# Four sums of squares from two rounded products each, a last token tile that ends in halves, and a new table of shifts

## The chip, the cores and the metric

The kernel runs on one core of a Trainium2 chip. The metric is the device time of one execution in microseconds (us); three timed runs of the kernel before are given below, and one further execution was profiled. TensorE (PE in the profile) multiplies, VectorE (DVE) and ScalarE (ACT) work on whole tiles of 128 partitions, GpSimd (POOL) and SyncE (SP) mostly start transfers. PEld is TensorE's loading of its stationary operand, which has its own records.

## The reference, cut to what matters

One layer of a diffusion backbone over 512 latent tokens and 256 context tokens, width 1024, all in float32:

```python
h = rms_norm(x, g_norm1) * (1.0 + sc1) + sh1
aq, ak, av, dq, dk, dv, dz, da, db, ga, gd = split_cols(h @ w_in)
y_attn = window_ctx_attention(q_a, k_a, v_a, k_ac, v_ac, attn_sink)
...
q_d, k_d, v_d = jnp.split(centred_short_conv(...), 3, axis=-1)       # with a silu
q_d = l2_normalize(heads(q_d, DN_HEADS)) * DN_HEAD_DIM ** -0.5       # 8 heads of 64
k_d = l2_normalize(heads(k_d, DN_HEADS))
o_dl, _, _ = bidir_delta(q_d, k_d, v_d, g, beta, s_cf, s_cb)         # chunks of 64 tokens
...
x_new = x + gt1 * (sigmoid(ga) * (y_attn @ w_br_attn) + sigmoid(gd) * (y_d @ w_br_dn)) @ w_out
out = x_new + gt2 * (square(relu(hm @ w_mlp1)) @ w_mlp2)
```

`l2_normalize` multiplies each head's 64 numbers with `rsqrt(sum of squares + 1e-6)`.

## The kernel before

**Layout.** Features stand on the 128 partitions and tokens along the columns until the last product. A product that needs float32 accuracy is made of three products of rounded operands (type fp32r): each operand is cut into an upper part `hi` and a rest `lo` by the helper `split` (one ACT copy with rounding, L231; one DVE subtraction, L232), and hi·hi, hi·lo and lo·hi are added up in one PSUM bank. A few small products are left in plain float32 (the trace has two records for each of them).

**The DeltaNet queries.** The 512 query features stand in four tiles `qT` of 128 x 512 (two heads each). In `rest`, `l2n` normalises one tile after another: ACT squares the tile (L785), one plain float32 product with `bones` (L788) sums the squares of each head, ACT takes Ln of the sums and Exp of minus half of it (L189), DVE multiplies the query with it (L795). `bones` is a 128 x 128 matrix of zeros and ones, one block of ones for each head; it is also used for the keys (`l2n` on 768 columns), for the attention's norms (L573) and for one sum of gates (L868).

**What runs beside it.** `rest` is woven with the four context steps of the DeltaNet recurrence (`chain_step`, whose products of 64 x 64 are at L1250), with the inversion of the triangular matrices on DVE (`invert`, L979 and L980) and with a `filler`: the products of the attention's branch (L1201) and of the gates (L1155). The eight latent steps of the recurrence follow, then the norm of its output (L1446), its transposes (L1451) and the product with `w_br_dn`.

**The last product.** `Flat.run` makes the last quarter of the MLP's second product: for each half `n` of the 1024 output columns, four banks `z` for four tiles of 128 tokens, and 4 pieces of weights x 2 x 3 products of 512 columns for each tile (L1876 to L1878). Each finished bank is multiplied with the gate's row (L1885), added to what the other three quarters left (L1887), and written to memory by SP (L1888).

**Order.** `arrange` lays the instructions of every engine in an order that is worked out when the program is built: `Lists.run` walks through them with its own costs and always takes the ready instruction of the lowest rank. The rank is the place in the program text, and each entry of `SHIFTS` (engine or -1 for all, first place, end, distance) moves the ranks of a range. Buffers come from one `Arena` that hands out places in a ring from `mem.ptr`; a place that is used again makes its new user wait for the old one.

Of the kernel before, what the change touches and what calls it, by code (L numbers as in the profile page):

```python
# [10 lines left out]
F32 = mybir.dt.float32  # L11
F32R = mybir.dt.float32r
BF16 = mybir.dt.bfloat16
AF = mybir.ActivationFunctionType
ALU = mybir.AluOpType
# [31 lines left out]
P = 128  # L47
D = 1024
KT = D // P
SEQ = 512  # L50
# [71 lines left out]
def tile_layer(ctx: ExitStack, tc: tile.TileContext, I: dict, out: bass.AP, dbg=None):  # L122
    nc = tc.nc
    V, A, G, PE = nc.vector, nc.scalar, nc.gpsimd, nc.tensor
# [5 lines left out]
    mats = ctx.enter_context(tc.tile_pool(name="mats", bufs=1))  # L130
# [5 lines left out]
    def nm(s):  # L136
        uid[0] += 1
        return f"{s}_{uid[0]}"

    mem = Arena(lambda o, n: nc.alloc_sbuf_tensor_at(nm("m"), [P, n], F32, offset=base + o * 4).ap(), 256, NU)  # L140
# [6 lines left out]
    alloc, bank = mem.get, lambda n=1: banks.get(n * 512)  # L147
# [3 lines left out]
    def load(out, key, *at):  # L151
        d = nc.sync.dma_start(out=out, in_=I[key][at] if at else I[key])
        if lastload:
            tie(d.ins, lastload[0].ins.name)
        return d

    def cload(key, shape, pool=const):
        t = pool.tile(list(shape), F32, name=f"c_{key}")
        load(t, key)
        return t  # L160
# [5 lines left out]
    r32 = lambda ap: ap.bitcast(F32R)  # L166
# [10 lines left out]
    def tie(later, name, how=nosync):  # L177
        tc.add_manual_dep(later, name, how, reason="order")
        ties.append((later.name, name))

    def act(out_, in_, func, **kw):

        sets = TABLES.get(func)
        if sets and actg["set"] not in sets:
            head = A.preload_act_table_set(sets[0])
            for o in actg["ops"]:
                tie(head.ins, o.name)
            actg.update(set=sets[0], head=head.ins, ops=[head.ins])
        r = A.activation(out_, in_, func, **kw)  # L189
        if sets:  # L190
            tie(r.ins, actg["head"].name)
            actg["ops"].append(r.ins)
        return r
# [258 lines left out]


    ident = cload("ident", [P, P], mats)
    bones = cload("bones", [P, P], mats)
    identb = mats.tile([P, P], BF16, name="identb")
    V.tensor_copy(identb, ident)
    maskb = mats.tile([P, 2, P], BF16, name="maskb")
# [77 lines left out]
    def wnext():  # L536
        w = wn.pop(0)
        if wq:
            wn.append(wq.pop(0)())
        return w  # L540
# [240 lines left out]
    def l2n(y, scale, parts, eps):  # L781

        n = parts[-1][1]
        t = alloc(n)
        A.activation(t.ap, y, AF.Square)  # L785
        for lo, hi in parts:
            ss = bank()
            PE.matmul(ss[:, :hi - lo], bones, t[:, lo:hi], start=True, stop=True)  # L788
            act(t[:, lo:hi], ss[:, :hi - lo], AF.Ln, bias=eps)
            ss.free()  # L790
        act(t.ap, t.ap, AF.Exp, scale=-0.5)
        if scale == 1.0:
            V.tensor_tensor(y, y, t.ap, op=ALU.mult)
        else:
            V.scalar_tensor_tensor(y, y, scale, t.ap, op0=ALU.mult, op1=ALU.mult)  # L795
        t.free()
# [10 lines left out]
    t, t2 = alloc(TOK), alloc(TOK)  # L807
# [249 lines left out]
    def mats():  # L1057
        for q in range(4):
            l2n(kT[q].ap, 1.0, ((0, SEQ), (SEQ, TOK)), epsc)
            yield  # L1060
        for gi in range(3):
            yield from chunk_mats(gi)
# [282 lines left out]
    def rest():  # L1345
        for q in range(4):
            l2n(qT[q].ap, HD ** -0.5, ((0, SEQ),), epsc4)
            yield
        for g in (1, 2):
            to_tokens(VTM, vT, g)  # L1350
            yield
        for t in vT:
            t.free()
        for g in (1, 2):
            to_tokens(KTM, kT, g)
            yield
# [18 lines left out]
    for g in range(2):  # L1375
        ms = slice(16 * g, 16 * g + 16)
        f, b = xa[0][:, ms], xa[1][:, ms]
# [9 lines left out]
    for g in range(2):  # L1387
# [20 lines left out]
        for a in range(2):  # L1408
            lo, hi = quad(a, 0), quad(a, 1)
# [38 lines left out]
    for qq in range(2):  # L1448
# [3 lines left out]
        for a in range(2):  # L1452
            n = 2 * qq + a
            t = alloc(512)
# [15 lines left out]
    for ct in range(8):  # L1470
        w = wnext()
# [32 lines left out]
    for ct in range(8 - NHALF):  # L1504
        w = wnext()
# [329 lines left out]
    class Flat:  # L1835
# [27 lines left out]
        def run(self):  # L1863

            self.ready.append(next(self.made))
            for n in range(2):
                z = [bank() for _ in range(4)]
                for p in range(4):
                    if len(self.parts) < 4:
                        self.left()  # L1870
                    hi, lo = self.parts[p]
                    wh, wl = self.ready.pop(0)
                    for tt, zz in enumerate(z):
                        c = slice(tt * P, tt * P + P)
                        for k in range(2):
                            PE.matmul(zz.ap, hi[:, k, c], wh[:, k], start=(p == k == 0), stop=False)  # L1876
                            PE.matmul(zz.ap, hi[:, k, c], wl[:, k], start=False, stop=False)  # L1877
                            PE.matmul(zz.ap, lo[:, k, c], wh[:, k], start=False, stop=(p == 3 and k == 1))  # L1878
                    m = next(self.made, None)
                    if m:  # L1880
                        self.ready.append(m)
                for tt, zz in enumerate(z):
                    cols, r = slice(n * 512, n * 512 + 512), tt % 2 * 512
                    y, t = alloc(512), ends[f"{1 + tt // 2}{1 + n}"][:, r:r + 512]
                    V.tensor_tensor(y.ap, zz.ap, grow[0][:, cols], op=ALU.mult)  # L1885
                    zz.free()
                    V.tensor_tensor(t, t, y.ap, op=(ALU.add, ALU.subtract)[n])  # L1887
                    nc.sync.dma_start(out=out[tt][:, cols], in_=t)  # L1888
                    y.free()

    def gather():

# [24 lines left out]
    ends = {}  # L1917
    grow = []
# [5 lines left out]
    for hf in range(4):  # L1924
        for f in range(0 if hf else FT):
            if first:
                bufs, _, acc = first.pop(0)
            else:
                bufs = [alloc(1024), alloc(1024)]
                w = wload(I["wm1"][f], bufs=bufs)  # L1930
                acc = bank()
                mm3(acc.ap.rearrange("p (n t) -> p n t", n=2), w, ms)
            r = alloc(512)
# [175 lines left out]
class Lists:  # L2109
# [177 lines left out]


SHIFTS = (
    (-1, 3553, 4764, 98), (-1, 3512, 3594, 1006), (-1, 7403, 7446, -155), (-1, 1987, 1996, 101), (0, 2046, 2292, -17),  # L2290
    (-1, 6044, 6077, -106), (0, 2023, 2126, -10), (-1, 115, 426, -27), (-1, 3445, 3672, -1637),
    (-1, 1527, 1528, 1489), (-1, 6310, 6694, -52), (-1, 1462, 1509, -625), (0, 2939, 2999, -93),
    (-1, 2608, 2663, 1010), (2, 3601, 4703, 34), (-1, 7250, 8101, -33), (0, 1850, 1939, 203), (-1, 2383, 2384, 17500),
    (-1, 3674, 3774, -4398), (0, 677, 698, -656), (-1, 3082, 3203, -110118), (-1, 2293, 2400, -38),
    (0, 6368, 6391, 130), (1, 4083, 4115, 18), (0, 2284, 2614, 138), (0, 2832, 2895, 504), (-1, 6541, 6601, -172),
    (1, 5748, 5839, -1941), (-1, 6770, 6908, 5), (0, 1571, 1968, -41), (-1, 82, 309, 175), (0, 6907, 7054, -30),
    (-1, 6985, 6999, 100), (0, 333, 759, 687), (2, 6255, 6839, 92), (-1, 2338, 2928, -326), (0, 5230, 5288, 60),
    (0, 6605, 6630, -34), (2, 6286, 6635, 1090), (0, 1833, 2823, -52), (-1, 3067, 3168, -1479), (0, 6835, 7284, -25),
    (-1, 6617, 6991, 6), (-1, 2334, 2705, -850), (1, 2045, 2628, 25751), (1, 2966, 3000, 88), (-1, 1888, 1979, 54),
    (-1, 6683, 6694, -12), (0, 4982, 5022, -19), (-1, 4895, 4909, -322), (2, 4328, 4389, -910), (2, 3659, 3660, -79),  # L2300
    (0, 3816, 4086, -547), (2, 3616, 3661, 426), (-1, 2698, 2889, -283), (-1, 791, 795, -1080), (-1, 4468, 4565, -70),
    (-1, 2662, 2768, 153), (0, 4688, 4730, 677), (-1, 1453, 2428, 57), (0, 3513, 3676, 1376), (-1, 2538, 2557, -85),
    (2, 3307, 3572, -734), (-1, 4301, 4316, 1562), (-1, 8021, 8081, -103), (0, 6446, 6490, -40), (-1, 6515, 6522, 73),
    (0, 4612, 4652, 330), (2, 2868, 2901, -688), (1, 6422, 6428, 63), (0, 7237, 7252, -31), (2, 3468, 3519, 1105),
    (0, 3385, 3512, -60), (0, 3767, 3844, -440), (-1, 3889, 4042, -388), (-1, 2356, 2379, -340), (0, 4054, 4254, -37),
    (1, 2710, 3030, -12), (-1, 3938, 4538, 65), (1, 1906, 1916, -331), (0, 2607, 2757, -420), (-1, 4509, 4514, 38),
    (1, 4064, 4220, -270), (0, 4178, 4479, -520), (0, 4039, 4130, 255), (0, 2791, 2991, -300), (1, 1978, 2978, -9),
    (-1, 7512, 8112, -45), (0, 1814, 1875, -81), (-1, 7228, 7238, -9), (0, 4201, 4254, 1120), (0, 4218, 4249, -885),
    (1, 3798, 4198, 186), (-1, 4320, 4327, -8), (0, 2876, 3156, 18), (0, 3295, 3371, -6), (-1, 3570, 4170, -472),
    (-1, 4087, 4267, -15), (-1, 2701, 2752, 63), (0, 3821, 4137, -80),  # L2310
)


# [120 lines left out]
```

## Time and profile before

| | us |
|---|---|
| median of three runs | 851.46 (850.16 to 853.5) |
| the profiled execution | 848.21 |
| its span, from the first to the last instruction | 846.4 |
| PE busy in the span | 833.7 |
| DVE busy | 699.2 |
| ACT busy | 534.2 |

The profiled execution has 1.81 us outside its span. PE is busy 98% of the span; PE records overlap one another (a record of 389 ns is followed by the next after some 227 ns), so where the profile gives the chain of work, the time from one product to the next is read there and not from the mean record. The granted clock is 1.00 in every 20 us of the span up to 840, which is TensorE's upper level of 2.4 GHz.

### The profile page before, as it was taken

What the parts mean: (1) busy time and instruction counts of PE and PEld (TensorE: products, weight loads), DVE (VectorE), ACT (ScalarE), POOL (GpSimd) and SP (SyncE); (2) the same over time, 40 slices, a digit from 0 to 9 for tenths busy, and PEclk for the clock granted to TensorE, in tenths of its full rate; (3) what the DMA queues carried; (4) which work ended last, traced back from release to release, by engine and by line L of the source; (5) the groups of instructions that cost most, each with busy time, mean ns of one, the idle gap of its engine ahead of it and who ended that gap; (6) DMA issues with size and microseconds to landing.
All of it is one profiled execution on the core that took longest, in us unless ns stands there. A gap on an engine that the chain in (4) does not pass through costs nothing.

```text
span 846.4 us, 18086 instructions
## 1 busy us (share of the span) xinstructions
PE 833.7 (98%) x7464; PEld 698.4 (83%) x7464; DVE 699.2 (83%) x1153; ACT 534.2 (63%) x920; POOL 60.3 (7%) x81
## 2 busy tenths in 40 slices
PE   8999999999999999999999999999999999999997
PEld 5688778887877778787778899888998899889986
DVE  5875999988779998868849879798689988989853
ACT  5568785487769896587754345398557447646520
POOL 0000011010000002000000000110011001111300
PEclk9999999999999999999999999999999999999999
DMA  9924365543221237643116755959259636998271
GB/s 367 369 76 100 76 151 124 124 85 70 38 38 31 62 116 243 213 141 103 41 41 246 241 161 190 312 131 264 95 157 194 169 129 162 187 269 229 35 190 50
DMA packets 38178, 127.31 MB, mean 150 GB/s; under 512 B 4688, under 2 KB 5200, under 8 KB 38096
## 3 DMA queue, kind: packets, MB, share of 16 engines
q1 hardware_dynamic: 30176, 99.43, 34.3%
q0 software_dynamic: 7920, 26.74, 18.6%
q8 instruction: 58, 0.95, 0.5%
q14 instruction: 24, 0.20, 0.1%
HBM read 118.29 MB, written 4.19 MB: 145 GB/s over the span
## 4 chain that ended last, share of the span: by engine, by line
PE 92%; DMA 5%; ACT 1%; DVE 1%; SPq 0%; issue 0%; ACTq 0%
PE banks L1619 14%; PE banks L1155 14%; PE banks L335 9%; PE banks L337 9%; PE banks L339 9%; PE banks L1809 4%; PE banks L1807 4%; PE banks L1808 4%; PE banks L1250 3%; PE banks L1201 3%; DMA m<-in_wada 2%; PE banks L732 2%; PE banks L1876 2%; PE banks L1878 2%; PE banks L1877 2%; DMA wr<-in_win 1%
## 5 line engine op out<-in xcount | busy, mean ns | idle before, releaser
L1619 PE MATMUL banks<-m,m 128*128 128x256 f32 x1008 | 126.2, 284 | 0.7 <-ACT m L231 0.7
L1619 PEld LDWEIGHTS banks<-m,m 128*128 128x128 f32 x1008 | 123.6, 192 | 2.9 <-ACT m L231 1.6
L231 ACT ACTIVATE m<-m 128x512 fp32r<-128x512 f32 (+2 forms) x123 | 90.9, 761 | 52.7 <-PE banks L1808 8.6
L232 DVE TENSOR_TENSOR m<-m,m 128x512 fp32r<-128x512 f32 (+2 forms) x123 | 103.0, 854 | 15.2 <-ACT m L231 12.9
L335 PE MATMUL banks<-m,wh 128*128 128x512 f32 (+1 forms) x312 | 112.1, 363 | 0.0
L337 PE MATMUL banks<-m,wh 128*128 128x512 f32 (+1 forms) x312 | 110.2, 355 | 0.0
L339 PE MATMUL banks<-m,wl 128*128 128x512 f32 (+1 forms) x312 | 109.6, 354 | 0.0
L1155 PE MATMUL banks<-m,wh 128*128 128x512 f32 x320 | 104.4, 401 | 1.3 <-ACT m L189 1.3
L299 ACT ACTIVATE wh<-wr 128x1024 fp32r<-128x1024 f32 (+1 forms) x60 | 56.6, 944 | 47.8 <-DMA wr<-in_wout 13.9
L1155 PEld LDWEIGHTS banks<-m,wh 128*128 128x128 f32 x320 | 59.2, 188 | 14.3 <-ACT m L189 1.8
L335 PEld LDWEIGHTS banks<-m,wh 128*128 128x128 f32 x312 | 58.9, 189 | 8.5 <-issue 0.5
L337 PEld LDWEIGHTS banks<-m,wh 128*128 128x128 f32 x312 | 59.0, 189 | 8.2 <-issue 0.5
L339 PEld LDWEIGHTS banks<-m,wl 128*128 128x128 f32 x312 | 58.9, 189 | 8.1 <-DVE wl L304 0.2
L1807 PE MATMUL banks<-wh,m 128*128 128x512 f32 x168 | 65.4, 392 | 0.0
L1808 PE MATMUL banks<-wl,m 128*128 128x512 f32 x168 | 65.2, 390 | 0.0
L1155 PE MATMUL banks<-m,wl 128*128 128x512 f32 x160 | 64.4, 404 | 0.4 <-DVE wl L304 0.4
L1809 PE MATMUL banks<-wh,m 128*128 128x512 f32 x168 | 64.4, 391 | 0.0
L304 DVE TENSOR_TENSOR wl<-wr,wh 128x1024 fp32r<-128x1024 f32 (+1 forms) x44 | 45.1, 1024 | 13.3 <-ACT wh L299 13.2
L335 PE MATMUL banks<-m,m 128*128 128x256 f32 (+1 forms) x136 | 45.6, 341 | 0.6 <-ACT m L344 0.5
L231 ACT ACTIVATE wh<-m 128x1024 fp32r<-128x1024 f32 x30 | 31.6, 1055 | 22.8 <-DMA m<-in_wm 15.5
L1733 POOL DMA_DIRECT2D m<-in_wm x24 | 20.8, 920 | 348.9 <-PE banks L339 167.2
L337 PE MATMUL banks<-m,m 128*128 128x256 f32 (+1 forms) x136 | 44.9, 337 | 0.1
(298 smaller groups left out, 1814.1 us busy)
## 6 DMA issues: line engine op xcount, KB each, us to landing
m<-in_wada SPq DMA_DIRECT2D x48, 512.0 KB, 5.0
wr<-in_win SPq DMA_DIRECT2D x38, 512.0 KB, 3.8
m<-in_wm SPq DMA_DIRECT2D x36, 512.0 KB, 4.9
wr<-in_wm SPq DMA_DIRECT2D x28, 512.0 KB, 4.5
m<-in_wm POOLq DMA_DIRECT2D x24, 512.0 KB, 7.6
wl<-in_win POOLq DMA_DIRECT2D x16, 512.0 KB, 6.0
m<-in_xT SPq DMA_DIRECT2D x8, 512.0 KB, 4.8
wr<-in_wbr SPq DMA_DIRECT2D x16, 256.0 KB, 2.6
```

Source lines behind the costliest of these rows:

```text
L231: A.activation(r32(hi), src, AF.Copy)
L232: (eng or V).tensor_tensor(r32(lo), src, hi, op=ALU.subtract)
L299: upper[0] = A.activation(r32(hi), raw, AF.Copy)
L304: V.tensor_tensor(r32(lo), raw, hi, op=ALU.subtract)
L335: PE.matmul(acc, w[0][:, k, :], xhi, start=(start and i == 0), stop=False)
L337: r = PE.matmul(acc, w[0][:, k, :], xlo, start=False, stop=(end and w[1] is None))
L339: r = PE.matmul(acc, w[1][:, k, :], xhi, start=False, stop=end)
L1155: PE.matmul(acc.ap, w[x][:, k, :], hx[k][y], start=(k == p == 0), stop=(k == KT - 1 and p == 2))
L1619: PE.matmul(dst, r32(self.w[w][i][:, k * P:(k + 1) * P]), xs7[x][k][j], start=(n == 0), stop=(n == 11))
L1807: PE.matmul(zz, hi[:, kk, ts_], wh[:, k], start=(kk == 0), stop=False)
L1808: PE.matmul(zz, hi[:, kk, ts_], wl[:, k], start=False, stop=False)
L1809: PE.matmul(zz, lo[:, kk, ts_], wh[:, k], start=False, stop=(kk == 3))
```

## The change

- `l2n` on 512 columns, the queries alone, cuts the squares into an upper part and a rest (`split`, into a place `up` that `aside` takes without moving the arena's pointer), and sums them by two fp32r products with `bones` (`head_sums`) in place of one float32 product. The keys' calls, with 768 columns, stay as they are.
- `bones` is loaded into a buffer of the arena and copied by ACT with the rounding type. Its load no longer goes through `load`, which ties a load behind the last of the `wada` loads.
- In the second half of `Flat.run` the last tile of 128 tokens has two banks of 256 columns instead of one of 512. Its 24 products of 512 columns become 48 of 256, and it is multiplied, added and written in two halves.
- `SHIFTS` is another table (99 entries after 103).

```diff
-    bones = cload("bones", [P, P], mats)
+    bones = mats.tile([P, P], F32, name="bones")
+    b_ = alloc(256)
+    nc.sync.dma_start(out=b_[:, :P], in_=I["bones"])
+    A.activation(r32(bones), b_[:, :P], AF.Copy)
+    b_.free()
+    def aside(n):
+        at = mem.ptr
+        b = alloc(n)
+        mem.ptr = at
+        return b
+    def head_sums(dst, hi, lo):
+        PE.matmul(dst, r32(bones), r32(hi), start=True, stop=False)
+        PE.matmul(dst, r32(bones), r32(lo), start=False, stop=True)
...
         A.activation(t.ap, y, AF.Square)
+        up = aside(2 * n) if n == SEQ else None
+        if up:
+            split(t.ap, up[:, :n], up[:, n:])
         for lo, hi in parts:
             ss = bank()
-            PE.matmul(ss[:, :hi - lo], bones, t[:, lo:hi], start=True, stop=True)
+            if up:
+                head_sums(ss[:, :hi - lo], up[:, lo:hi], up[:, n + lo:n + hi])
+            else:
+                PE.matmul(ss[:, :hi - lo], bones, t[:, lo:hi], start=True, stop=True)
...
-                z = [bank() for _ in range(4)]
+                z = [bank() for _ in range(4 + n)]
...
+                        if n and tt == 3:
+                            for h, zz in ((slice(0, 256), z[3]), (slice(256, 512), z[4])):
+                                for k in range(2):
+                                    PE.matmul(zz[:, :256], hi[:, k, c], wh[:, k, h], start=(p == k == 0), stop=False)
+                                    PE.matmul(zz[:, :256], hi[:, k, c], wl[:, k, h], start=False, stop=False)
+                                    PE.matmul(zz[:, :256], lo[:, k, c], wh[:, k, h], start=False, stop=(p == 3 and k == 1))
+                            continue
...
+                    w = 256 if n and tt == 3 else 512
+                    for o in range(0, 512, w):
+                        cols, t = slice(n * 512 + o, n * 512 + o + w), ends[f"{1 + tt // 2}{1 + n}"][:, at + o:at + o + w]
+                        V.tensor_tensor(y[:, o:o + w], z[tt + o // 256][:, :w], grow[0][:, cols], op=ALU.mult)
+                        V.tensor_tensor(t, t, y[:, o:o + w], op=(ALU.add, ALU.subtract)[n])
+                        nc.sync.dma_start(out=out[tt][:, cols], in_=t)
...
 SHIFTS = (
-    (-1, 3553, 4764, 98), (-1, 3512, 3594, 1006), (-1, 7403, 7446, -155), (-1, 1987, 1996, 101), (0, 2046, 2292, -17),
...
+    (-1, 3520, 4770, 98), (0, 7434, 7460, -59), (-1, 1995, 1996, 114), (-1, 2051, 2666, -45), (0, 2023, 2257, -108),
...
```

For the highest places the table before has `(-1, 8021, 8081, -103)`, the new one `(-1, 8046, 8342, -150)`; each `l2n` of a query, `bones` and the last tile together add some 40 instructions to the program.

## Rows read from the trace of the kernel before

**Rows 1.** The page: busy time by engine, and the chain's shares by engine.

```profile
PE 833.7 (98%) x7464; PEld 698.4 (83%) x7464; DVE 699.2 (83%) x1153; ACT 534.2 (63%) x920; POOL 60.3 (7%) x81
...
PE 92%; DMA 5%; ACT 1%; DVE 1%; SPq 0%; issue 0%; ACTq 0%
```

**Rows 2.** Busy time in four stretches, columns in the first line.

```profile
core 0: us, PE busy (x) PEld busy (x) DVE busy (x) ACT busy (x) POOL busy (x), PEclk, DMA share, GB/s
0.00:45.00 45.00, 40.38 (x290) 27.43 (x291) 31.93 (x73) 24.68 (x44) 0.21 (x4) 1.00 0.88 346
259.00:300.00 41.00, 40.26 (x331) 30.72 (x330) 39.97 (x72) 36.74 (x74) 0.00 (x0) 1.00 0.23 64
...
819.90:841.70 21.80, 21.79 (x97) 17.70 (x95) 8.38 (x11) 2.12 (x2) 0.00 (x0) 1.00 0.21 83
841.70:846.40 4.70, 0.00 (x0) 0.00 (x0) 1.38 (x2) 0.00 (x0) 0.00 (x0) 0.89 0.14 56
```

**Rows 3.** The chain in order of time: start us, us, line, products.

```profile
275.60 0.86 PE banks L788 x2
...
280.06 1.91 PE banks L788 x4
...
290.26 0.86 PE banks L788 x2
...
348.60 1.73 PE banks L901 x122
...
425.93 13.94 PE banks L1155 x60
...
601.93 32.75 PE banks L1619 x273
```

**Rows 4.** Timeline of ACT, PE and DVE, 259 to 300 us: start, us.

```profile
259.80 0.63 ACT L785 ACTIVATE m<-m 128x512 f32<-128x512 f32 x1
...
275.44 1.02 PE L788 MATMUL banks<-m,c_bones 128*128 128x512 f32 x2
...
293.95 0.68 DVE L795 SCALAR_TENSOR_TENSOR m<-m,m 128x512 f32<-128x512 f32 x1
```

**Rows 5.** Groups by form on ACT and DVE: count, busy us, mean ns.

```profile
L231 ACT ACTIVATE m<-m 128x512 fp32r<-128x512 f32 x76 | 46.3, 625 | 40.0 <-DMA m<-in_wm 8.4 <-DVE m L1610 8.3 <-DVE m L1477 6.1
...
L232 DVE TENSOR_TENSOR m<-m,m 128x512 fp32r<-128x512 f32 x76 | 51.1, 685 | 5.3 <-ACT m L231 4.8
...
L1307 DVE TENSOR_TENSOR m<-m,banks 128x256 f32<-128x256 f32 x20 | 8.1, 418 | 8.5 <-PE banks L1250 8.4
...
L1633 DVE TENSOR_TENSOR m<-m 128x256 f32<-128x256 f32 x12 | 5.0, 419 | 0.0
```

**Rows 6.** Timeline of the end of the span.

```profile
837.65 0.69 DVE L1885 TENSOR_TENSOR m<-banks,m 128x512 f32<-128x512 f32 x1 [2.66 <-PE banks L1878]
...
841.30 0.39 PE L1878 MATMUL banks<-wh,m 128*128 128x512 f32 x1
841.73 0.69 DVE L1885 TENSOR_TENSOR m<-banks,m 128x512 f32<-128x512 f32 x1 [2.66 <-PE banks L1878]
842.45 0.69 DVE L1887 TENSOR_TENSOR m<-m,m 128x512 f32<-128x512 f32 x1
...
843.17 0.33 SPq L1888 DMA_DIRECT2D out<-m  x1
```

**Rows 7.** Transfers from 842.4 to 846.4 us, 40 slices of 0.1 us.

```profile
GB/s 0 0 0 0 0 0 0 0 0 0 0 0 0 0 0 0 369 389 369 389 492 389 205 21 0 0 0 0 0 0 0 0 0 0 0 0 0 0 0 0
...
out<-m SPq DMA_DIRECT2D x1, 256.0 KB, 2.0
```

**Rows 8.** Timeline of PE and DVE after the recurrence, 414 to 452 us.

```profile
423.68 1.16 PE L1250 MATMUL banks<-m,m 64*64 64x64 f32 x64
...
439.71 0.71 PE L1451 MATMUL banks<-c_ident,m 128*128 128x128 f32 x5
...
430.88 2.36 DVE L1446 TENSOR_TENSOR m<-m,oss 128x1024 f32<-128x1024 f32 x2 [0.65 <-ACT oss L189]
```

## What the change will do: the prediction

> **What bounds the kernel now.** I read the page's totals first. PE is busy 833.7 of 846.4 us, and the chain that ended last runs 92% through PE [rows 1]. So the first question is not which engine to relieve but where PE stands still, and how much PE work the change removes. The windows answer the first half. Of the 846.4 − 833.7 = 12.7 us without a product, 45.00 − 40.38 = 4.6 lie in the first 45 us, where the DMA engines are 88% busy and the core waits for its inputs, and 4.7 lie behind the last product [rows 2]. That leaves 3.4 us in 797. In the middle, then, a microsecond of PE work that goes away is a microsecond of span, as long as no other engine has become the next limit there. DVE is the candidate: in the 41 us in which the queries are normalised it is busy 39.97 us, and ACT 36.74 [rows 2].
>
> Two paces are needed, and both come from the chain in order of time, since records overlap. Products of 512 rounded columns follow each other by 13.94 / 60 = 0.232 us with their neighbours' disturbances, and by 21.80 / 96 = 0.227 in the undisturbed last half [rows 2, 3]. Products of 256 columns, each with a stationary operand of its own, go by 32.75 / 273 = 0.120 us [rows 3].
>
> **The sums of squares.** One float32 product over 512 columns is two records and takes 0.86 us of the chain; there are four: 0.86 + 1.91 (two together) + 0.86 = 3.63 us [rows 3]. The pair in the middle lies between two groups of 64 x 64 products, and some 0.19 of its 1.91 is above two single ones: that is switching, which may stay. So 3.44 to 3.63 us go. Eight products of 512 rounded columns come, at 0.232: 1.86 us. PE has 1.6 to 1.8 us less to do; I take 1.7.
>
> Each query also gets an ACT copy of 0.625 us and a DVE subtraction of 0.685 [rows 5]: 2.5 and 2.7 us in all, in a stretch where ACT had 4.3 us free and DVE 1.0 [rows 2]. Two things could wait for that. First the product itself, which stands in PE's order with everything else behind it. In the trace a query's square starts at 259.80 and its product at 275.44, 15 us later [rows 4]; the next three have 13 to 20 us. The 1.3 us more fit in. The last scaled query is there at 294 and the products that need the queries start at 348.6 [rows 3, 4]. Second, the inversion, with which these subtractions share DVE: it ends up to 2.7 us later, and with it the latent recurrence. That recurrence has cover. Its last products come at 423.68 + 1.16 = 424.8, the norm of its output is done at 430.88 + 2.36 = 433.2, and the transposes that need it stand at 439.71, behind gate products that fill PE meanwhile [rows 8]. So 6.5 us of delay cost nothing, and I cost the DVE work at nothing. Without that cover it would cost 2.7.
>
> **Bones.** The load is the same 64 KB; the rounding copy has 128 columns, less than the 0.625 us of 512 [rows 5], and falls in the first 45 us or just behind, where ACT is busy 24.68 of 45 us [rows 2]. Nothing, then. Losing the tie to the `wada` loads matters only if SP puts this load ahead of one of them: at 346 GB/s [rows 2], 64 KB are 0.2 us. That is the upper bound.
>
> **The last tile.** On PE 24 x 0.227 = 5.45 us become 48 x 0.120 = 5.76: +0.31. Behind the last product the trace has the multiplication at 841.73, the addition at 842.45, and SP's issue at 843.17 [rows 6]: two DVE operations of 0.69 in a row. With 256 columns they take 0.42 each [rows 5], so −0.54, if the first half is out of the way. The evictions show that it is: they stand 841.73 − 837.65 = 4.08 us apart [rows 6], that is 18 products of 0.227 and not 6, so the order finishes a tile's last three weight pieces before it turns to the next tile. If the new order treats the two halves likewise, the first is finished 18 x 0.120 = 2.2 us before the end, and its 0.84 us of DVE work and its own SP issue of 0.33 are over by then. If the halves end together instead, four operations of 0.42 take 1.68 where two took 1.41: +0.27 instead of −0.54. The new table moves the program's end forward as the old one does, so I take −0.54. The last transfer moves 256 KB in 0.75 us (seven and a half slices), out of 2.0 from issue to landing [rows 7]; half the bytes give −0.37 at this pace, and nothing if the pace halves with the shorter rows. I take −0.37. The fifth bank is the one that the first half of the columns leaves first; it is wanted 18 products, 4.1 us, into the second half, and one DVE operation of 0.69 frees it [rows 6]: nothing.
>
> The tail is −0.54 − 0.37 + 0.31 = −0.6 us, between −0.6 and +0.6.
>
> The 273 products at 0.120 us each have a load of the stationary operand of their own [rows 3], and a load's record is 17.70 / 95 = 0.186 us [rows 2], so the loads lie under the products. A rule speaks against that and against the change. The Trainium skill, in "TensorE: Matmul & The Clock Gate", section "Part 3: Packing small matmuls — row/col tiling", says that loads overlap running products only when their row groups differ, which whole-array products don't; its section "LDWEIGHTS (loading the stationary operand)" gives 128/1.2, about 107 ns, for a load, so that 24 further loads would cost an estimated 2.6 us and the sum would be about +0.3 instead of −2.3. The trace's pace of 0.120 doesn't agree with that rule; it agrees with Part 2 of the same page, which also lets a load run ahead into a background buffer.
>
> **The shifts.** This is the cost that no row shows. The new order can at best win the 3.4 us that PE stands still in the middle; the 4.6 us at the start are bound by the bytes of the inputs. It can lose wherever a product is put ahead of its operand, and at the start, where a 512 KB load that is put ahead of a needed one costs 0.5 MB / 346 GB/s = 1.5 us [rows 2]. No row says which of the two tables fits the chip better. I take zero, in the middle between ends that lie alike far off, and ±2 us around it.
>
> **Sum.** −1.7 − 0.6 = −2.3 us. Against the profiled execution's own 848.21 that is 845.9. The three runs' median, 851.46, stands 3.25 above that execution, more than the change is worth; moved by the same −2.3 it is 849.2, and that is my number, a ratio of 0.9973. Half a per cent, 4.3 us, is about what a measurement of this kernel can tell from no change, so the likeliest verdict is no change.
>
> **Rivals.**
>
> *The new order also wins the idle time.* PE's 3.4 us in the middle go too: −5.7, 845.8 us. For it: outside the start and the tail nothing but the order keeps PE waiting. Against it: there is little left to win, and it would have to win more than 2.0 of the 3.4 to pass half a per cent. Chance 0.17, most of it beyond that line.
>
> *PE isn't what sets the time there.* DVE is 97% busy in that stretch and gets 2.7 us more [rows 2, 5]. If what PE gains is given back at the next wait for DVE, only the tail stays: −0.6, 850.9 us. Against it: the 6.5 us of cover. Chance 0.12.
>
> *Slower: the recurrence comes late.* One mechanism: the new order lays the inversion and the recurrence so that the last group of 64 x 64 products falls behind its 424.8. Up to 6.5 us later costs nothing [rows 8]; from there each microsecond is one of span with PE standing still before the transposes. Past 6.5 + 2.3 = 8.8 us the kernel is slower than before, past 13 by over half a per cent. DVE's 2.7 us alone don't reach the first of these points, but from 348.6 to 424.8 [rows 3, 8] the recurrence and what it needs are 76 us of handed-on steps. At 13 us: 855.7 us. Chance 0.08.
>
> *The loads of the halves aren't hidden.* Then 24 x 0.186 = 4.5 us more stand in the tail [rows 2], +2.2 in all: 853.7 us. Against it: the pace of 0.120 [rows 3]. It is the rule of the Trainium skill's Part 3, above, as a mechanism. Chance 0.02.
>
> **How the numbers follow.** The forecast has the rest, 0.61, with ±2 us of its own from the order and the tail. Faster by over 0.5%: 0.14 of the first rival and 0.03 from the forecast's edge, 0.17. Slower by over 0.5%: the late recurrence, 0.08, and 0.01 for a disturbed start: 0.09. Within: 0.74. The range reaches down to 845.0, which takes in the first rival's time, and up to 853.0, past the second; outside lie the slower case, the loads and the edges.
>
> **What would show it.** In the changed kernel's profile: eight products with `bones` of about 0.23 us in the chain and no float32 pair of 0.86 for the queries; the four subtractions on DVE, and an inversion that ends up to 2.7 us later while the transposes at L1451's new line still follow PE work; the last tile at a pace of 0.12; the 1.5 us from the last product's end at 841.7 to SP's last issue become 0.9; a last transfer that lands in about 1.6. PE busy should fall by 1 to 2 us. The forecast is wrong if the idle time of PE in the middle is far from 3.4 us, if the start of the first weight tile moves, or if the transposes wait for the recurrence.

## The result, and the profile after

The changed kernel takes 854.74 us (median of 14 runs, 851.8 to 859.7); the kernel before, in 14 runs beside it, 850.27 (848.8 to 854.05). The ratio is 1.0050, with a 95% interval of 1.0036 to 1.0065: 4.5 us slower by the medians, where −2.3 was forecast and 853.0 was the range's upper end. The profiled execution after took 854.03 us with a span of 852.3. That of before, 848.21, is the fastest of all its runs here, so the two profiles stand 5.8 us apart, 1.3 more than the medians. (The table of shifts has 92 entries after 100, not 99 after 103 as said above.)

The page after answers to [rows 1]; the windows and the transfer at the end answer to [rows 2, 7]:

```profile
PE 836.1 (98%) x7488; PEld 700.8 (82%) x7488; DVE 702.2 (82%) x1159; ACT 535.8 (63%) x925; POOL 59.9 (7%) x81
...
PE 83%; DVE 6%; DMA 5%; ACT 4%; issue 1%; DVEq 0%; ACTq 0%
```

```profile
0.00:45.00 45.00, 40.46 (x284) 26.73 (x285) 31.26 (x73) 24.69 (x44) 0.21 (x4) 0.96 0.89 346
...
848.30:852.30 4.00, 0.00 (x0) 0.00 (x0) 0.85 (x2) 0.00 (x0) 0.00 (x0) 0.85 0.26 98
...
out<-m SPq DMA_DIRECT2D x1, 128.0 KB, 1.8
```

PE has less to do and is busy 2.4 us longer; the chain, 92% PE before, now goes through DVE and ACT for a tenth of its length. Behind the last product stand 4.0 us where 4.7 stood. Of the queries' sums, the chain in order of time (start us, us, line) shows what was forecast, rounded products of 0.23 (of the eight, one starts with 0.26 and two stand at 0.43); DVE's timeline of the end answers to [rows 6]:

```profile
278.89 0.26 PE banks L469
279.15 0.23 PE banks L470
...
286.38 0.43 PE banks L469
```

```profile
846.89 0.69 DVE L1919 TENSOR_TENSOR m<-m,m 128x512 f32<-128x512 f32 x1
848.31 0.42 DVE L1918 TENSOR_TENSOR m<-banks,m 128x256 f32<-128x256 f32 x1 [0.73 <-PE banks L1904]
848.77 0.42 DVE L1919 TENSOR_TENSOR m<-m,m 128x256 f32<-128x256 f32 x1
```

So the edits look right one by one, and the time was lost elsewhere. Where, the same windows of before and after show (columns as in [rows 2]: length, then PE, PEld, DVE, ACT, POOL busy). Before:

```profile
260.00:300.00 40.00, 39.26 (x326) 29.93 (x325) 38.97 (x70) 35.74 (x72) 0.00 (x0) 1.00 0.23 66
300.00:340.00 40.00, 40.00 (x722) 32.06 (x721) 35.58 (x59) 31.48 (x67) 5.18 (x10) 1.00 0.58 184
340.00:380.00 40.00, 39.46 (x743) 31.29 (x745) 30.46 (x59) 27.57 (x65) 3.12 (x6) 1.00 0.55 176
700.00:740.00 40.00, 40.00 (x247) 36.13 (x247) 38.14 (x45) 27.79 (x33) 6.93 (x8) 1.00 0.82 181
780.00:820.00 40.00, 40.00 (x248) 35.87 (x247) 29.68 (x41) 18.76 (x26) 7.10 (x8) 1.00 0.44 95
```

After:

```profile
260.00:300.00 40.00, 38.65 (x296) 30.23 (x295) 39.50 (x69) 37.91 (x79) 0.00 (x0) 1.00 0.23 66
...
340.00:380.00 40.00, 38.79 (x732) 30.53 (x732) 31.70 (x59) 28.19 (x65) 4.51 (x9) 1.00 0.57 188
700.00:740.00 40.00, 38.26 (x247) 34.57 (x247) 34.69 (x43) 26.44 (x32) 6.15 (x8) 1.00 0.73 161
780.00:820.00 40.00, 39.55 (x263) 36.17 (x262) 30.05 (x40) 21.64 (x28) 7.11 (x8) 1.00 0.45 105
```

PE stands still 0.6 us more at 260 to 300, 0.7 at 340 to 380, 1.7 at 700 to 740 and 0.5 at 780 to 820: 3.5 of the 5.9 us between the spans, and 0.6 more lie at 45 to 260 us. The other 2.4 are PE's longer busy time, and the tail gives 0.7 back. In this execution the start takes 1.6 of the 2.4: the granted clock is 0.96 over the first 45 us where before has 1.00, on 40.46 us of PE work. That clock is not the reason for the loss: five of the changed kernel's runs have a mean granted clock of 1.00, and their median is 854.72 too. Which other records are longer, and why, isn't settled.

### The profile page after: what moved, and what is told of

Same layout as the page of the kernel before. It is cut to its first block, busy times and chain, and to the rows that moved or that the text cites. A ratio compares the mean times of both kernels' runs of the same rounds, so it can differ in the third digit from the quotient of the medians.

```text
span 852.3 us, 18149 instructions
## 1 busy us (share of the span) xinstructions
PE 836.1 (98%) x7488; PEld 700.8 (82%) x7488; DVE 702.2 (82%) x1159; ACT 535.8 (63%) x925; POOL 59.9 (7%) x81
## 4 chain that ended last, share of the span: by engine, by line
PE 83%; DVE 6%; DMA 5%; ACT 4%; issue 1%; DVEq 0%; ACTq 0%
PE banks L1179 12%; PE banks L335 10%; PE banks L337 9%; PE banks L339 9%; PE banks L1643 8%; PE banks L1833 4%; PE banks L1832 4%; PE banks L1831 4%; DMA m<-in_wm 3%; PE banks L1274 3%; PE banks L1225 3%; PE banks L748 2%; PE banks L1908 1%; PE banks L1909 1%; PE banks L1907 1%
## 5 line engine op out<-in xcount | busy, mean ns | idle before, releaser
L231 ACT ACTIVATE m<-m 128x512 fp32r<-128x512 f32 (+2 forms) x127 | 93.2, 757 | 54.6 <-DVE m L1634 13.2
L232 DVE TENSOR_TENSOR m<-m,m 128x512 fp32r<-128x512 f32 (+2 forms) x127 | 106.0, 851 | 16.6 <-ACT m L231 12.7
L335 PE MATMUL banks<-m,m 128*128 128x512 f32 (+1 forms) x136 | 45.7, 343 | 0.5 <-ACT m L344 0.3
L337 PE MATMUL banks<-m,m 128*128 128x256 f32 (+1 forms) x136 | 44.8, 336 | 0.0
```

What stands on the lines that cost most here:

```text
L231: A.activation(r32(hi), src, AF.Copy)
L232: (eng or V).tensor_tensor(r32(lo), src, hi, op=ALU.subtract)
L335: PE.matmul(acc, w[0][:, k, :], xhi, start=(start and i == 0), stop=False)
L337: r = PE.matmul(acc, w[0][:, k, :], xlo, start=False, stop=(end and w[1] is None))
```

## The experiments

Two things had been priced at zero: the shifts, and the splits' work on ACT and DVE. In the kernels below the table of shifts is replaced by a list of all instructions, so that the order can be chosen apart from the edits:

```diff
 def settled(lists):
-    rank = list(range(lists.n))
...
-    return lists.run(rank)[0]
+    return ORDER
```

"Before's order" means that the instructions of before keep their sequence on every engine; the new ones stand beside the ones they belong to.

**The order alone, in whole and in halves.** The kernel before without any edit, in the changed kernel's sequence on every engine.

> The kernel before, none of the edits, its instructions in the order that the changed kernel gives them. If the order is what costs: the whole loss and the edits' gain on top, +4.3 + 2.3 = +6.6 us (1.0078). If the edits cost: within 1 us of the kernel before.

Measured: 856.82 us against 849.93, ratio 1.0071 (1.0051 to 1.0091). The shifts alone cost at least as much as the whole change, by the medians more (the intervals overlap). Its windows:

```profile
260.00:300.00 40.00, 38.65 (x290) 29.29 (x289) 36.67 (x65) 34.45 (x72) 0.00 (x0) 1.00 0.22 66
...
340.00:380.00 40.00, 37.88 (x728) 29.72 (x727) 31.29 (x59) 28.00 (x64) 4.66 (x10) 1.00 0.62 193
700.00:740.00 40.00, 39.12 (x255) 35.50 (x254) 35.15 (x44) 27.03 (x32) 6.43 (x8) 1.00 0.72 160
780.00:820.00 40.00, 38.67 (x261) 35.72 (x260) 30.04 (x40) 21.63 (x28) 7.12 (x8) 1.00 0.45 104
```

PE loses time at the same four places as in the changed kernel: 0.6, 1.6, 0.9 and 1.3 us more idle than before. Its 7464 products, those of before, are also busy 2.2 us longer (835.9 us), with the granted clock at 1.00; which records and why isn't settled. At two of the places the waits point at loads. At 320 to 440 us DVE waits for loads of `wada` (us, times, longest): the late modulation's sums stand in DVE's order ahead of their loads, and the recurrence's steps stand behind them. Here, and then in the changed kernel, where before has 2.1 us:

```profile
DVE m L518 <- DMA m<-in_wada: 6.5, 4, 2.2
```

```profile
DVE m L534 <- DMA m<-in_wada: 4.3, 6, 1.2
...
ACT wh L231 <- DMA m<-in_wm: 4.7, 3, 2.2
...
PE banks L1831 <- ACT m L231: 1.4, 1, 1.4
```

The last two lines are the changed kernel's at 700 to 745 us: ACT waits 4.7 us (before 2.2) for loads of `wm` to split, and PE then waits 1.4 for a split of the activations that ACT does behind it; before's PE waits for nothing there.

The length of such a wait alone is no loss: new_order_second_half, below, keeps before's order at 340 to 380 us, its DVE waits 4.4 us for `wada`, and its PE stands still no longer than before's. What counts is the chain. Before's has no load at 340 to 380 us nor at 700 to 740; with the new order alone, loads of `wada` are 27% of it in the one stretch and loads of `wm` 30% in the other, in the changed kernel 10% and 24%. The two pieces of `wada` in the new order's chain:

```profile
339.30 5.38 DMA m<-in_wada
...
348.25 6.14 DMA m<-in_wada
```

No kernel moved these loads by themselves, so that they are the cause is argued, not shown. The profile also has PE idle at 340 to 360 us with no wait that it can name, in six of the kernels here and not in before: 0.9 us in this one, 1.6 and 2.0 in new_order_first_half and before_copies_subtractions below. What causes that is open.

The next two kernels have that order only in the first part, up to about 500 us, or only behind it:

> The program of before, none of the edits; the instructions that come first in before's order, up to about 500 us, stand in the changed kernel's order, the rest in before's. Theory (the order costs by separate places that each hold PE, and nothing later gives it back): the places before 500 us stay and those after go. In the profile of new_order_alone the products stand 3.2 us further behind before's at 440 to 500 us and 6.5 behind at the end, so this kernel loses 3.2 us, ratio 1.0038, with DVE waiting for the loads of the late modulation between 340 and 380 us as there, and no gap at 720 to 740. Rival 1 (the loss is one late thing, the split behind an accumulating load at 710 to 730 us and what follows): ratio 1.000. Rival 2 (a delay in the first half is absorbed by slack in the second): ratio under 1.001 although the gap at 360 to 380 is there.

> The complement: before's order up to about 500 us, the changed kernel's order behind it, none of the edits. Theory: the 6.5 - 3.2 = 3.3 us of the second half, ratio 1.0039, 1.6 of it at 720 to 740 us (PE waits for the split of a weight tile that stands on ACT behind a copy that waits for an accumulating load) and 1.6 at 800 to 820. The two halves together give the 1.0071 of new_order_alone. Rival 1 (all of it is late): 1.007. Rival 2 (the second half only suffers because it is entered late): 1.000.

Measured: 1.0057 (1.0038 to 1.0076) and 1.0048 (1.0035 to 1.0061). Both halves lose, so no single late wait is the cause, and a delay in the first isn't absorbed by the second. Their sum, 1.0105, is above 1.0071. The seam between two orders may cost something by itself: in the first of the two PE stands still 0.75 us at 500 to 520 us, where before has no idle time. That wasn't tried alone.

**The edits in before's order, a first try.**

> All edits, but every engine keeps the order that it has in the kernel before; the new instructions stand beside those that they belong to. If the order of the new table is what costs: -2.3 us against the kernel before, as the sum of the edits has it (ratio 0.9973, between 0.995 and 0.999). If the edits themselves cost (DVE subtractions beside the inversion, places of buffers): +4 us (1.005), as in the changed kernel.

> The sums of squares and the copy of bones alone, in the order of the kernel before. If the order is what costs: -1.7 us (0.998). If DVE's four subtractions or the places of the new buffers cost: +3 to +5 us (1.004 to 1.006).

> The last tile in halves alone, in the order of the kernel before. Forecast's sum: -0.6 us (0.9993), of which the part behind the last product falls from 4.7 to 3.8 us. If the loads of the halves show: +2 us or more.

Measured: all edits 1.0111 (1.0097 to 1.0125), sums alone 1.0081 (1.0069 to 1.0093), tail alone 1.0034 (1.0022 to 1.0046). Two things in how these kernels were laid out add to it. `aside` gives each query's `up` a place that overlaps that of the query before. In before's order the squares run far ahead of the products, so each square now waits for the previous query's second product, L470, as ACT's timeline of the sums shows:

```profile
278.38 0.63 ACT L801 ACTIVATE m<-m 128x512 f32<-128x512 f32 x1 [0.20 <-PE banks L470]
...
285.23 0.63 ACT L801 ACTIVATE m<-m 128x512 f32<-128x512 f32 x1 [0.17 <-PE banks L470]
```

PE is busy for 3.2 of the 7 us from 280 to 287, and for the 6.8 us after that the granted clock is at its lower level, 1.2 GHz.

And in before's order the tile `tt == 3`, the one that is halved, is finished first and not last. Its second half's eviction came at the very end, behind a whole tile's:

```profile
848.94 0.69 DVE L1895 TENSOR_TENSOR m<-m,m 128x512 f32<-128x512 f32 x1
849.55 0.41 DVE L1894 TENSOR_TENSOR m<-banks,m 128x256 f32<-128x256 f32 x1
850.00 0.42 DVE L1895 TENSOR_TENSOR m<-m,m 128x256 f32<-128x256 f32 x1
```

That is a part of the 2.9 us that the tail alone loses, 0.6 of it behind the last product (5.3 us where before has 4.7). PE also waits 0.8 us for a weight's split ahead of the halves, and in the profiled execution the granted clock is 0.74 at 20 to 40 us; the rest is open.

**The tail, repaired.** The edit of `Flat.run` alone; in the list the halved tile (`tt == 3`) takes the place of the tile that before's order finishes last (`tt == 2`), which moves into its place:

```diff
-                z = [bank() for _ in range(4)]
+                z = [bank() for _ in range(4 + n)]
...
-    return lists.run(rank)[0]
+    return ORDER
```

> Only the last tile's halves, in before's order, the halves being those of the tile that before's order finishes last (in old_order_tail they were of the one that it finishes first). No bones, no splits. Theory: -0.6 us, ratio 0.9993, from the last product's end to the span's end 0.8 to 0.9 us less than before's 4.7, products of 256 columns at 0.12 us. Rival 1 (the loads of the halves are not hidden): +2.2, ratio 1.0026. Rival 2 (any change at all to this order loses 3 to 5 us): 1.004 to 1.005.

Measured: 849.54 against 849.92, ratio 0.9993 (0.9981 to 1.0004): the forecast was −0.6 us, and the interval holds both that and no change. PE's timeline shows halves that start 0.12 us apart, so their loads, with records of 0.19 us, don't show as time; DVE's shows that the first half is out of the way:

```profile
844.13 0.28 PE L1879 MATMUL banks<-wl,m 128*128 128x256 f32 x1
844.25 0.28 PE L1880 MATMUL banks<-wh,m 128*128 128x256 f32 x1
...
842.87 0.43 DVE L1895 TENSOR_TENSOR m<-m,m 128x256 f32<-128x256 f32 x1
844.57 0.42 DVE L1894 TENSOR_TENSOR m<-banks,m 128x256 f32<-128x256 f32 x1 [1.27 <-PE banks L1880]
```

**The sums, repaired.** Each query's `up` has 512 columns at a place of its own, and the rest replaces the squares:

```diff
-        up = aside(2 * n) if n == SEQ else None
+        up = apart(n) if n == SEQ else None
...
-            split(t.ap, up[:, :n], up[:, n:])
+            under = mem.at(t.start * 256, n)
+            split(t.ap, up.ap, under)
```

> Sums of squares and rounded bones alone, in before's order and with places of their own as in edits_old_order_apart, last tile as before. Theory: -1.7 us, ratio 0.9980, and 0.6 us slower than edits_old_order_apart. Rival (the splits' 5.2 us of ACT and DVE work delay what PE needs next): 1.000 to 1.005, with PE idle between 280 and 320 us.

> All the edits (rounded bones, two products per query, the last tile's halves) in before's order, which every instruction of before keeps on PE, DVE, ACT, POOL and SP. Two things differ from old_order_all: the split of each query's squares has 512 columns of its own at a place that neither the other queries nor a neighbour in time uses (the rest replaces the squares in place), and the halves are of the tile that before's order finishes last. Theory (the edits are worth what the sum of instructions says, and old_order_all lost by a wait that the shared place of the splits made and by halves in the wrong tile): -2.3 us, ratio 0.9973, products with bones at 275 to 300 us without PE idle before them, and the last product to the span's end about 0.7 us shorter than before. Rival (the edits cost more than they remove in whatever order, for instance because DVE and ACT take the splits from something on the path): ratio over 1.000.

Measured: sums 1.0049 (1.0037 to 1.0061), all edits 1.0057 (1.0043 to 1.0070). The repair was worth 2.7 us of the sums' loss (1.0081 to 1.0049), and the theory that the shared place was the whole loss falls. The 2.7 are the wait and the lower clock behind it together, and the raw copy of `bones` lies at another place too; no run tells these apart. The sums alone, window and PE's waits (258 to 300 us):

```profile
260.00:300.00 40.00, 35.19 (x246) 26.22 (x245) 37.04 (x65) 34.05 (x68) 0.00 (x0) 1.00 0.16 42
```

```profile
PE banks L1182 <- ACT m L189: 1.7, 1, 1.7
PE banks L1065 <- DVE m L772: 1.3, 1, 1.3
PE banks L1228 <- DVE wl L304: 0.6, 1, 0.6
```

PE stands still 4.8 us where before it stands 0.7, and not at the sums: products of the gates (L1182) wait for an activation, transpositions (L1065) for a multiplication of the attention's result, products of the attention's branch (L1228) for a weight's split. The splits of the squares are new on ACT and DVE ahead of them; the next three kernels ask whether that is the cause.

**The splits' load by itself.** Before with four subtractions, four copies, or both, beside its float32 products:

```diff
         A.activation(t.ap, y, AF.Square)
+        if n == SEQ:
+            up = apart(n)
+            A.activation(up.ap, t.ap, AF.Copy)
+            V.tensor_tensor(up.ap, t.ap, up.ap, op=ALU.subtract)
+            up.free()
```

> The kernel before in its own order, with its four float32 products with bones, and four more DVE subtractions of 128x512 (one behind each query's square, at the place in DVE's order that the split has in sums_old_order_apart, their result read by nobody). It tells whether DVE's time by itself is what the sums of squares lost in before's order: there PE stood still for 4.8 us between 260 and 300 us where before it stands for 0.7, and the chain of waits goes through DVE and ACT from 257 to 291 us. Theory (DVE sets the pace there, and each of the 0.68 us is one of span): +2.7 us, ratio 1.003, with PE idle 3 to 4 us between 260 and 300. Rival 1 (it is ACT's four copies, or the handover from ACT to DVE to PE): within 0.5 us, ratio 1.000. Rival 2 (any change at all to this order loses 4 to 5 us, wherever it is): 1.005.

> The kernel before in its own order with four more ACT copies of 128x512, one behind each query's square at the place where sums_old_order_apart splits; nobody reads them. before_four_subtractions lost 1.8 us by DVE's share alone (ratio 1.0021); with the subtractions on POOL 1.0040 stayed, which points at ACT. Theory (ACT's copies hold up what DVE and PE take from ACT there): +1.5 to +2.5 us, ratio 1.002 to 1.003. Rival (ACT had 4 us free in that stretch and hides them): 1.000.

> Both: four copies and four subtractions, as the split makes them, beside the four float32 products of before. Theory (the two loads add up, and are all that the sums of squares lost): sums_old_order_apart lost 4.1 us although PE's work was 1.7 less, so the loads cost 5.8: ratio 1.006 to 1.007. Rival (the new products or the wait for the second of them have a part in the loss): 1.004 or less.

Measured: subtractions 1.0021 (1.0010 to 1.0033), copies 1.0021 (1.0009 to 1.0033), both 1.0063 (1.0048 to 1.0078). Each is worth about 1.8 us by itself and the two 5.4, as much as the 2.5 + 2.7 us of work that the prediction had counted and taken for hidden. That the two cost more than the sum of each isn't clear of the noise; by the traces they add up: the last of the recurrence's transpositions here (L1038 of before) starts at 298.3 us in before, at 300.9 with the subtractions (which are 0.3 late already ahead of the stretch), at 300.6 with the copies and at 302.8 with both, so 2.3, 2.3 and 4.6 us late. With both, PE's window at 260 to 300 us is like that of the sums, with the old products:

```profile
260.00:300.00 40.00, 35.92 (x244) 26.32 (x243) 37.05 (x65) 33.99 (x67) 0.00 (x0) 1.00 0.17 42
```

**The rest on POOL.** `split(t.ap, up.ap, under, eng=G)`.

> As sums_old_order_apart, but the four subtractions that make the rest are on POOL, which has nothing to do there between 253 and 320 us, instead of DVE. Theory (DVE sets the pace): PE's idle time between 260 and 300 us goes back towards 0.7, and the 1.7 us of PE work come out: ratio 0.998 if ACT's copies are hidden, up to 1.001 if each of their 0.63 us counts as well. Rival (what counts is the longer chain from a square to its product, or ACT): 1.003 to 1.005, as with DVE. POOL's time for such a subtraction is in no trace so far; the squares stand 13 to 20 us ahead of their products, which would hide one of several us.

> All the edits in before's order as in edits_old_order_apart, the rest of the squares on POOL. Theory: 0.6 us less than sums_rest_on_pool, ratio 0.997 to 1.000, a version that would beat both kernels at the lower end. Rival: 1.003 to 1.005.

Measured: 1.0040 (1.0025 to 1.0056) and 1.0039 (1.0027 to 1.0052). Lower than on DVE by 0.8 and 1.5 us, within the intervals, so a gain isn't shown. POOL takes 1.3 to 1.4 us each, and two DVE operations that start beside POOL's, each with two inputs from SBUF, end only 0.4 to 0.54 us behind it. The timelines of POOL and DVE:

```profile
269.92 2.85 POOL L232 TENSOR_TENSOR m<-m,m 128x512 fp32r<-128x512 f32 x2 [2.35 <-ACT m L231]
276.01 1.34 POOL L232 TENSOR_TENSOR m<-m,m 128x512 fp32r<-128x512 f32 x1 [3.24 <-ACT m L231]
...
271.58 1.73 DVE L232 TENSOR_TENSOR m<-m,m 128x512 fp32r<-128x512 f32 x1 [1.22 <-ACT m L231]
...
276.23 1.52 DVE L1007 TENSOR_TENSOR m<-m,m 128x368 f32<-128x368 f32 x1
```

**The new order where the splits are, and nowhere else.**

> All the edits (splits at places of their own, halves of the tile that is finished last); the changed kernel's order only for what before's order does between about 240 and 330 us, before's order elsewhere. Theory A (the new order was made to fit the splits in, and does: in that stretch it spreads squares and splits so that DVE and ACT don't hold PE, and it loses only outside it): the edits' -2.3 us and +0.4 for what new_order_alone lost in that stretch: -1.9 us, ratio 0.998, PE idle under 1.5 us between 260 and 300. Rival B (the order as a whole depends on itself, so that a piece of it in the other loses at its borders): +2 or more, ratio over 1.002. Rival C (the splits cost 4 to 5 us wherever they stand, and the gain of the changed kernel over new_order_alone came from elsewhere): 1.003 to 1.005.

> As edits_new_order_240_330, with the window's end at 312 us, since new_order_alone starts to lose ground between 320 and 340. Theory A: -2.0 us, ratio 0.9976. Rivals B and C as there.

Measured: 1.0023 (1.0009 to 1.0037) and 1.0018 (1.0007 to 1.0029), against 1.0057 for the same edits in before's order all through. The new order does hide the splits in the stretch that it was made for: PE's idle time at 260 to 300 us is 1.4, not 4.8. Part of it comes back behind that stretch. The kernel with the window to 312 us:

```profile
260.00:300.00 40.00, 38.63 (x329) 30.30 (x327) 39.49 (x70) 37.16 (x76) 0.00 (x0) 1.00 0.24 67
300.00:340.00 40.00, 37.85 (x725) 30.27 (x714) 36.04 (x62) 30.46 (x66) 5.08 (x10) 1.00 0.52 165
340.00:380.00 40.00, 37.99 (x699) 30.05 (x697) 30.17 (x56) 27.24 (x62) 3.21 (x7) 1.00 0.55 175
```

2.2 us at 300 to 340, where the chain goes through the inversion on DVE, and 2.0 at 340 to 380 (before 0.0 and 0.5). Of the first, 1.9 us are one wait of PE for DVE, close to the end of the stretch; of the second, 1.5 are idle time for which the profile names no wait. Of the theories, A was right on the idle time at 260 to 300 us and too low on the ratio, C too high; B, a loss at the borders with a ratio over 1.002, comes nearest, with the two ratios at its edge.

**PE's gain without any load.** The rest is left out; ACT writes the square rounded, and one rounded product sums it:

```diff
-        A.activation(t.ap, y, AF.Square)
+        sq = mem.at(t.start * 256, n) if n == SEQ else None
+        A.activation(t.ap if sq is None else r32(sq), y, AF.Square)
...
+                PE.matmul(ss[:, :hi - lo], r32(bones), r32(sq[:, lo:hi]), start=True, stop=True)
```

> Leaves out the rest of the squares: ACT's square is written rounded, one product of 512 rounded columns per query (with rounded bones) takes the place of the float32 product, no copy and no subtraction is added; before's order, last tile as before. It tells whether PE's work at this place is worth its time when nothing is put on DVE and ACT. Theory (PE's share of the sum was right, the loads on DVE and ACT were what was mispriced): 4 x (0.86 - 0.23) = -2.5 us, ratio 0.997. Rival (with DVE and ACT nearly full there, PE only waits longer for its next operand): 0.999 to 1.000, with PE idle 1.5 to 3 us more than before's 0.7 between 260 and 320.

> The same together with the halves of the tile that is finished last (tail_old_order_last, 0.9993); leaves out the rest of the squares. Theory: -2.5 - 0.6 = -3.1 us, ratio 0.9964. Rival: -0.6 to -1.2, ratio 0.9986 to 0.9993.

Measured: 1.0000 (0.9991 to 1.0010), and with the tail 0.9991 (0.9978 to 1.0004). 2.5 us of PE work are gone, nothing was added, and nothing is gained. The windows of the first, and its chain at 276 to 278 us:

```profile
260.00:300.00 40.00, 38.12 (x323) 29.28 (x322) 39.02 (x71) 35.83 (x72) 0.00 (x0) 1.00 0.22 65
...
340.00:380.00 40.00, 38.34 (x725) 30.53 (x724) 28.94 (x55) 26.81 (x62) 3.11 (x6) 0.96 0.51 165
```

```profile
276.16 0.63 DVE m L988
...
276.81 0.63 DVE m L989
...
277.46 0.65 DVE m L988
```

The gain is given back inside the stretch. This execution is 0.3 us behind before's at 260 us, and the last of the recurrence's transpositions starts at 298.4 us, in before at 298.3: of the 2.5 us, 0.2 are left. PE stands still 1.1 us more than before at 260 to 300. (The 1.1 us more at 340 to 380, with the granted clock at 0.96, come behind that.) Where before's chain goes through PE at 274 to 290 us [rows 3], this one goes from DVE operation to DVE operation from 273.8 to 286.8, most of them the inversion's (L988 and L989 here). PE and DVE had been level there, and with 2.5 us less on PE, the chain is DVE's.

## Why the prediction was wrong

**The step that failed** is "I take zero, in the middle between ends that lie alike far off, and ±2 us around it", on the shifts. The new order costs 6.0 us by itself (1.0071). The bounds were too tight as well; in its trace the loss is several small ones between 260 and 820 us, none of the idle times that were added above 2 us, and 2.2 us of longer PE records. In that order the edits bring some 1.8 us (1.0050 against 1.0071, with intervals that overlap), near the forecast's 2.3, but the difference isn't clear of the noise.

**The step behind it** is "I cost the DVE work at nothing". In before's order the splits' load costs 5.4 us. The cover I had named, 6.5 us before the transposes, is at the recurrence's far end, and the load was felt long before that: PE stood still at the first products whose operands were late, at 260 to 300 us, and the filler further on in its list wasn't pulled forward. [rows 2] had DVE free for 1.0 us of 41, and I read that as a limit for DVE alone. So the new table was no arbitrary reshuffle: where it stands in for before's order at 240 to 312 us, PE's idle time at 260 to 300 falls from 4.8 to 1.4 us. That its losses elsewhere are the price of that isn't shown; the kernels with a window came to +1.5 to +2 and not to −2.

**"In the middle, then, a microsecond of PE work that goes away is a microsecond of span"**, with DVE as the candidate for the next limit. The candidate was right and the rule wrong: 2.5 us of PE work were worth nothing, with an interval from −0.8 to +0.9 us. This is the rival "PE isn't what sets the time there", to which I gave 0.12. Its time, 850.9, supposed that the gain is given back, and not that the load costs on top.

**The sums' PE terms** were right: eight products of 0.23, no pair of 0.86. **The tail** was right: 0.42 + 0.42 on DVE, 4.0 us instead of 4.7 behind the last product, and 0.9993 alone, which the runs can't tell from no change. Its transfer lands in 1.8, not 1.6, so half the bytes gave 0.2 and not 0.37. **The loads of the halves** are hidden, as the pace of 0.12 had said. The rule of the Trainium skill's "TensorE: Matmul & The Clock Gate", Part 3, that loads overlap running products only where the row groups differ, doesn't agree with this trace: halves start at 844.13 and 844.25, closer than a load's record of 0.19 us is long. **Bones** can't be told from zero: one_rounded_product has the rounded copy in it and stands at 1.0000. **The late recurrence** in the form I gave it, free up to 6.5 us and then at the transposes, didn't come. **The other rival**, idle time won by the order, had the wrong sign.

No version beat the kernel before by more than its measurement tells; the tail by itself (0.9993) and with one rounded product (0.9991) come lowest.

## What to carry to other kernels

Here PE was 98% busy, DVE 97% and ACT 90% in the same stretch, and each of them was a bound: 2.5 us of work taken from PE were worth nothing, and work given to DVE or ACT cost nearly its full length there (2.3 us of 2.7 and of 2.5). With shares like these, expect a gain on one engine to be given back to the next, and added work on any of them to show. Cover counts only if it stands in the engine's list between the late operand and the product that needs it, so name the first product that waits and not the last. And price a rewritten order by running it without the edits, and the edits without it, before adding the two up.

## What the runs showed of the hardware

A POOL subtraction of 128x512 held up DVE: DVE's own subtraction of that size took 1.73 us where it takes 0.685 [rows 5], ending only behind POOL's at 272.8, and one over 368 columns 1.52 where others in the same trace take 0.54. The Trainium skill, "SBUF — State Buffer", section "🔬 SBUF: two separate sides", says that DVE with two SBUF inputs and a GpSimd instruction that reads SBUF lock one another out for the whole instruction; the trace agrees.

Work added on two engines that feed PE added up: between 262 and 300 us, 2.7 us more on DVE put PE's products 2.3 us back, 2.5 us more on ACT 2.3, and both together 4.6.

The granted clock changed with what PE did: in old_order_sums PE was busy for 3.2 of 7 us at 280 to 287, and for the next 6.8 us the clock was at 1.2 GHz instead of 2.4.
